# Dilated attention: the dense result's reload and a head's first merge weight tied to their program place

## The chip, the cores and the metric

The kernel runs on one core of a Trainium2 chip (trn2), as one program. The time is that of the whole program on the device, in microseconds (us), and lower is better. Engines are named as the profile names them: PE is TensorE (PEld its weight loads), ACT ScalarE, DVE VectorE, POOL GpSimd, SP SyncE. Each engine runs its own instructions in a fixed order; a queue that issues DMAs (transfers) belongs to an engine and stands in that same order.

## The reference

The whole kernel is a block of a transformer over 2048 positions: projections of the input, a differential attention of 4 heads, a dilated attention of 8 heads of width 64, an output projection, and then a second block with sliding-window attention. The change lies in the dilated attention. It computes, for each head, three banded attentions whose keys stand 1, 4 and 16 positions apart, and mixes them by their softmax denominators:

```python
DIL_PATTERNS = ((128, 1), (512, 4), (2048, 16))

def dilated_attention(q, k, v, slopes):
    """Mixture of dilation patterns merged by their softmax denominators."""
    outs, lses = [], []
    for window, dilation in DIL_PATTERNS:
        o, lse = dilated_branch(q, k, v, slopes, window, dilation)
        outs.append(o)
        lses.append(lse)
    w = jax.nn.softmax(jnp.stack(lses, axis=0), axis=0)
    out = jnp.sum(w[..., None] * jnp.stack(outs, axis=0), axis=0)
    return out.astype(q.dtype)
```

## The kernel before

The kernel is written with a tile scheduler: the program is traced instruction by instruction, and the scheduler (`schedule_with_timeline_sim=True`) then puts the instructions of each engine in an order of its own, by an estimate of when each will be ready. Data dependences become semaphores. What a line of the program issues can therefore stand far from its place in the program.

The dilated attention is `phase_b2` (from L473), at about 1320 to 1735 us of the span. It runs a software-pipelined loop over n, 16 steps for each of 8 heads. A head has two results. The dense one ("nat": window 128, distance 1) has scores in L563, exponentials in L569, transposes in L603, a copy `d_pn` (L606), a split into high and low parts on POOL (L610, L611), the product with the values `d_vn` (L637), an evacuation by ACT (`d_ta`, L643), transposes back (L649) and a reduction on DVE (L650) into `d_o1`. The residue one ("res": the patterns of distance 4 and 16) has scores in L590, biases and minima in L593, exponentials in L595, transposes `d_tr` in L622, high parts `d_ph` on ACT (L624), low parts `d_pl` on DVE (L625), the product with `d_vr` (L733), and goes by the same evacuation and reduction into `d_o2`.

The two results have their rows in different orders. So the dense one takes a round trip through memory: `back_nat` stores it (L656, on ACT's queue) and `load_merge` reloads it in the order of the residue classes into `d_a1` (L660, on ACT's queue too), with four loads of a gate, `d_sz`, on SP's queue (L664). Then `weights` makes the merge weights out of the minima and sums of both results, with `d_mm` first (L685, DVE), and puts the merge's products on a list, from which the loop takes one per step: four products on POOL in L701, two sums in L718, two products with the gate in L719, and the stores L672.

In the program, head h is stored at step n = 16h + 21, reloaded at 16h + 33 (16h + 24 for the last head) and weighed at 16h + 38. The first sum of L718 is at step 16h + 42. `d_a1`, `d_sz` and `d_o2` have two buffers each, so that the reduction L650 of head h + 2 (step 16h + 47) writes where head h's `d_o2` was. The loads of the next head's keys and queries, of `d_vn` (L544) and of `d_vr` are issued on SP's queue at fixed steps of the loop. DMAs share a few semaphores, so one may be held back until an earlier one on the same semaphore has landed.

Of the kernel before, what the change touches and what calls it, by code (L numbers as in the profile page):

```python
# [11 lines left out]
ALU = mybir.AluOpType  # L12
# [4 lines left out]
P = 128  # L17
# [455 lines left out]
def phase_b2(tc, c, scr, nat_bias, res_bias, res_two):  # L473
    nc = tc.nc
    NS = 8 * NT
    with (
# [180 lines left out]

        def load_merge(h):
            a1 = op.tile([P, NT, 66], F32, name="d_a1")
            nc.scalar.dma_start(a1.rearrange("r (j g) w -> r j (g w)", g=4),  # L660
                                scr["o1"][h].rearrange("(j r g) w -> r j (g w)", r=P, g=4))
            sz = op.tile([P, NT, 64], F32, name="d_sz")
            for j in range(4):
                nc.sync.dma_start(sz[:, 4 * j:4 * j + 4], by_rows(scr["sz"][:, 512 + 64 * h:576 + 64 * h], j))  # L664
            mrg[h] = [a1, sz]

        def by_rows(ap, j):
            return ap[512 * j:512 * j + 512].rearrange("(r g) d -> r g d", g=4)

        def store_y(h, av):  # L670
            for j in range(4):
                nc.gpsimd.dma_start(by_rows(scr["y"][1 + h // 6][:, 64 * (h % 6):64 * (h % 6) + 64], j),  # L672
                                  av[:, 4 * j:4 * j + 4])

        def weights(h):
            a1, sz = mrg.pop(h)
            o2 = o2s[h]
            m2, l2 = m2s.pop(h)
            m1, l1 = a1[:, :, 64], a1[:, :, 65]

            def small(nm):
                return sp.tile([P, NT], F32, name=nm, bufs=2)

            mm, d1, d2, ll, lt = (small(nm) for nm in ("d_mm", "d_d1", "d_d2", "d_ll", "d_lt"))
            nc.vector.tensor_tensor(mm, m1, m2, ALU.min)  # L685
            nc.vector.tensor_sub(d1, mm, m1)
            nc.vector.tensor_sub(d2, mm, m2)
            nc.scalar.activation(d1, d1, AF.Exp)
            nc.scalar.activation(d2, d2, AF.Exp)
            nc.vector.tensor_mul(ll, l1, d1)  # L690
            nc.vector.tensor_mul(lt, l2, d2)
            nc.vector.tensor_add(ll, ll, lt)
            nc.vector.reciprocal(ll, ll)
            nc.vector.tensor_mul(d1, d1, ll)
            nc.vector.tensor_mul(d2, d2, ll)
            av = a1[:, :, 0:64]
            sd = op.tile([P, NT, 64], F32, name="d_sd", tag="d_o2") if h == 7 else None
            hs = (slice(0, NT // 2), slice(NT // 2, NT))

            def scale(x, ap, w):  # L700
                nc.gpsimd.tensor_mul(ap[:, x], ap[:, x], w[:, x].unsqueeze(2).broadcast_to([P, NT // 2, 64]))  # L701

            if h == 7:
                nc.gpsimd.tensor_mul(sd, sz, d2.unsqueeze(2).broadcast_to([P, NT, 64]))
                nc.vector.tensor_mul(av, av, d1.unsqueeze(2).broadcast_to([P, NT, 64]))
                nc.vector.tensor_mul(av, av, sz)

                def tail():
                    nc.vector.tensor_mul(o2, o2, sd)
                    nc.vector.tensor_add(av, av, o2)  # L710
                    store_y(h, av)

                later.append(tail)
                return
            later.extend([
                *[lambda x=x: scale(x, av, d1) for x in hs],
                *[lambda x=x: scale(x, o2, d2) for x in hs],
                *[lambda x=x: nc.gpsimd.tensor_add(av[:, x], av[:, x], o2[:, x]) for x in hs],  # L718
                *[lambda x=x: nc.gpsimd.tensor_mul(av[:, x], av[:, x], sz[:, x]) for x in hs],  # L719
                lambda: store_y(h, av),  # L720
            ])
# [27 lines left out]
        for n in range(NS + LEAD + LB + 12):  # L749
            r = n - LEAD  # L750
# [14 lines left out]
            for h in range(8):  # L765
                at = NT * (h + 1) + LN + DN + (BACK if h < 7 else 3)
                if n == at:
                    load_merge(h)
# [6 lines left out]
            for h in range(8):  # L775
                if n == NT * (h + 1) + (WT if h < 7 else LEAD + LB + DR + 3):
                    weights(h)
# [3 lines left out]
            h, t = divmod(n, NT)  # L781
# [592 lines left out]
```

## Time and profile before

| what | value |
|---|---|
| median of 3 runs | 3005.81 us (3000.62 to 3008.73) |
| the profiled execution | 2996.59 us |
| its span, first to last instruction | 2994.8 us |
| its mean granted TensorE clock | 0.985 |
| busy: PE, PEld, DVE, ACT, POOL | 97%, 82%, 60%, 52%, 41% |

All rows come from the one profiled execution, which is 9.2 us shorter than the median of the runs. Busy shares are means over the whole span, with stages of different limits in it. A row of a timeline gives start, duration, engine, line and operation, and in brackets how long the engine stood idle just before it and what it waited for. "DMA s_o<-d_o" is the store of the dense result, "DMA d_a<-s_o" its reload. The granted clock is given as a share of the full one, so 1.00 is 2.4 GHz and 0.50 is 1.2 GHz.

### The profile page before, as it was taken

The numbers are of one execution on the slowest core, as the hardware profiler recorded it, in microseconds if no ns is written. First come the engines' busy times: TensorE is split into PE (matmuls) and PEld (weight loads), VectorE is DVE, ScalarE is ACT, GpSimd is POOL, SyncE is SP. The second block draws the span as 40 slices with busy tenths as digits, with TensorE's granted clock in tenths as the row PEclk, the third lists the DMA queues.
The fourth block names the chain that finished last, engine by engine and source line by source line (L and its number), as shares of the span: only waits on it lengthen the run. The fifth ranks groups of instructions, "written<-read, shape, count | busy, mean of one in ns | idle before, by whom it ended". The sixth has DMA issues, their size and how long they took to land.

```text
span 2994.8 us, 45167 instructions
## 1 busy us (share of the span) xinstructions
PE 2891.2 (97%) x15554; PEld 2464.7 (82%) x15554; DVE 1802.8 (60%) x4607; ACT 1565.5 (52%) x3480; POOL 1240.2 (41%) x1156
## 2 busy tenths in 40 slices
PE   9999999999999999998898899999999999999998
PEld 7778888888788888888787778888788888888787
DVE  4115656522788889877676654444535756766755
ACT  5222333311688888877787642222345666666621
POOL 1110111101688888845676610000145665555421
PEclk9999999999999999999999899999999999999999
DMA  6653444414223322148666452322554343332452
GB/s 211 118 155 85 120 114 120 112 65 142 91 56 90 82 60 77 44 110 166 131 144 126 126 159 83 111 93 92 183 162 153 98 132 110 101 117 71 142 192 78
DMA packets 410645, 346.00 MB, mean 116 GB/s; under 512 B 89744, under 2 KB 356400, under 8 KB 408496
## 3 DMA queue, kind: packets, MB, share of 16 engines
q1 hardware_dynamic: 388000, 329.24, 39.3%
q10 hardware_dynamic: 20736, 8.65, 1.5%
q0 software_dynamic: 1680, 5.21, 0.7%
q8 instruction: 124, 2.03, 0.3%
q14 instruction: 105, 0.86, 0.1%
HBM read 227.51 MB, written 116.52 MB: 115 GB/s over the span
## 4 chain that ended last, share of the span: by engine, by line
PE 85%; DMA 6%; DVE 3%; ACT 2%; SPq 1%; issue 1%; POOL 1%; ACTq 0%; DVEq 0%; POOLq 0%
PE psm L190 8%; PE psm L192 8%; PE psm L191 8%; PE s_ps L331 7%; PE e_mm L803 5%; PE e_mm L805 5%; PE e_mm L804 5%; PE c_mm L803 4%; PE c_mm L804 4%; PE c_mm L805 4%; PE t_ps L375 3%; DMA s_o<-d_o 2%; PE o_ps L389 2%; PE o_ps L391 2%; PE o_ps L390 2%; PE f_mm L804 2%
## 5 line engine op out<-in xcount | busy, mean ns | idle before, releaser
L190 PE MATMUL psm<-w,hh 128*128 128x512 f32 x1024 | 406.1, 398 | 9.8 <-DVE t L111 8.0
L191 PE MATMUL psm<-w,hl 128*128 128x512 f32 x1024 | 399.9, 392 | 0.0
L192 PE MATMUL psm<-w,hh 128*128 128x512 f32 x1024 | 399.8, 393 | 0.0
L101 POOL TENSOR_TENSOR w<-wraw,w 128x512 fp32r<-128x512 f32 x64 | 81.7, 1296 | 599.0 <-ACT w L100 591.2
L365 POOL TENSOR_TENSOR et<-et 128x1024 f32<-128x1024 f32 x124 | 296.4, 2416 | 0.0
L331 PE MATMUL s_ps<-kst,qst 128*128 128x512 f32 x1024 | 289.3, 406 | 4.6 <-DVE mx L337 3.6
L347 ACT ACTIVATE et<-et,nm 128x2048 f32<-128x2048 f32 x128 | 257.3, 2010 | 5.2
L1025 POOL TENSOR_TENSOR e_wt<-e_raw,e_wt 128x1024 fp32r<-128x1024 f32 x80 | 191.3, 2399 | 111.5 <-ACT e_wt L1024 110.6
L190 PEld LDWEIGHTS psm<-w,hh 128*128 128x128 f32 x1024 | 193.5, 189 | 48.6 <-DVE t L111 8.4
L803 PE MATMUL e_mm<-e_x,e_wt 128*128 128x512 f32 x576 | 228.2, 396 | 1.1 <-DVE e_k L1067 0.9
L805 PE MATMUL e_mm<-e_x,e_wt 128*128 128x512 f32 x576 | 226.9, 394 | 0.0
L192 PEld LDWEIGHTS psm<-w,hh 128*128 128x128 f32 x1024 | 193.1, 189 | 40.8
L804 PE MATMUL e_mm<-e_x,e_wt 128*128 128x512 f32 x576 | 226.6, 393 | 0.0
L191 PEld LDWEIGHTS psm<-w,hl 128*128 128x128 f32 x1024 | 193.7, 189 | 38.3
L331 PEld LDWEIGHTS s_ps<-kst,qst 128*128 128x128 f32 x1024 | 176.2, 190 | 43.8 <-DVE mx L337 17.7
L1126 POOL TENSOR_SCALAR e_es<-e_es,e_l 128x256 f32<-128x256 f32 (+1 forms) x256 | 118.4, 481 | 170.6 <-DVE e_l L1124 108.5
L364 POOL TENSOR_SCALAR et<-et,cc 128x1024 f32<-128x1024 f32 x124 | 138.6, 1134 | 109.2 <-PE psm L192 57.1
L377 DVE TENSOR_TENSOR ptl<-t_ps,pth 128x512 fp32r<-128x512 f32 x256 | 169.2, 684 | 17.6 <-ACT pth L376 17.1
L337 DVE CUSTOM_DVE_ANT_0 et<-s_ps,nd,mx 128x1024 f32<-128x1024 f32 x128 | 163.8, 1280 | 26.5 <-PE s_ps L331 24.6
L1113 DVE CUSTOM_DVE_ANT_0 e_es<-e_s,e_bias,e_sk 128x256 f32<-128x256 f32 (+1 forms) x256 | 117.4, 472 | 102.7 <-PE e_s L1105 71.3
L376 ACT ACTIVATE pth<-t_ps 128x512 fp32r<-128x512 f32 x256 | 143.8, 596 | 42.7 <-PE t_ps L375 39.0
L337 DVE CUSTOM_DVE_ANT_0 et<-s_ps,nd 128x1024 f32<-128x1024 f32 x128 | 156.1, 1219 | 14.3 <-PE s_ps L331 7.0
(268 smaller groups left out, 7727.6 us busy)
## 6 DMA issues: line engine op xcount, KB each, us to landing
e_raw<-in_a_w_in_dram SPq DMA_DIRECT2D x80, 512.0 KB, 3.6
wraw<-in_w_in_dram SPq DMA_DIRECT2D x64, 256.0 KB, 3.5
kst<-s_dk SPq DMA_DIRECT2D x128, 128.0 KB, 4.0
s_xt<-c_at SPq DMA_DIRECT2D x32, 512.0 KB, 6.9
e_x<-s_xt SPq DMA_DIRECT2D x32, 512.0 KB, 7.7
t<-in_x_dram SPq DMA_DIRECT2D x32, 256.0 KB, 5.6
s_dv<-t SPq DMA_DIRECT2D x32, 256.0 KB, 3.2
s_bv<-t SPq DMA_DIRECT2D x32, 256.0 KB, 3.7
```

The lines of the kernel that those rows point to most:

```text
L190: nc.tensor.matmul(ps, ah, cur[k][:, 0], start=k == 0, stop=False)
L191: nc.tensor.matmul(ps, al, cur[k][:, 0], start=False, stop=False)
L192: nc.tensor.matmul(ps, ah, cur[k][:, 1], start=False, stop=k == KD - 1)
L331: nc.tensor.matmul(ps[:, b * 512:b * 512 + 512], lhs, heads[h, "k", e, i, 2 * hf + b], start=i == 0, stop=i == 1)
L337: nc.vector.tensor_tensor_reduce(et[:, hf], ps, bias[:, off:off + 1024], 1.0, -3.0e38 if hf == 0 else mx[:, 0:1], ALU.add, ALU.max, mx[:, ...
L347: nc.scalar.activation(ev, ev, AF.Exp, bias=nm, scale=slope, accum_out=st[g]["l"][:, e:e + 1])
L365: nc.gpsimd.tensor_sub(es[0][:, hf], es[0][:, hf], es[1][:, hf])
L377: nc.vector.tensor_sub(tl[:, :, qi], pt, th[:, :, qi].bitcast(F32))
L803: nc.tensor.matmul(ps, ah, bh, start=first, stop=False)
L804: nc.tensor.matmul(ps, al, bh, start=False, stop=False)
L805: nc.tensor.matmul(ps, ah, bl, start=False, stop=last)
L1025: nc.gpsimd.tensor_sub(w[:, 1], raw, w[:, 0].bitcast(F32))
```

## The change

Two calls are wrapped in `tc.keep_in_program_order`: the reload of the dense result in `load_merge` and the first merge weight in `weights`. A wrapped instruction stays behind everything that the program issues before it on its own engine; no wait for data comes with that. Both kernels have the same instructions. The scheduler lays the others out around the two, so the order changes on all engines, from head 0's reload on.

```diff
--- before.py
+++ after.py
@@ -657,8 +657,9 @@
 
         def load_merge(h):
             a1 = op.tile([P, NT, 66], F32, name="d_a1")
-            nc.scalar.dma_start(a1.rearrange("r (j g) w -> r j (g w)", g=4),
-                                scr["o1"][h].rearrange("(j r g) w -> r j (g w)", r=P, g=4))
+            tc.keep_in_program_order(nc.scalar.dma_start(
+                a1.rearrange("r (j g) w -> r j (g w)", g=4),
+                scr["o1"][h].rearrange("(j r g) w -> r j (g w)", r=P, g=4)))
             sz = op.tile([P, NT, 64], F32, name="d_sz")
             for j in range(4):
                 nc.sync.dma_start(sz[:, 4 * j:4 * j + 4], by_rows(scr["sz"][:, 512 + 64 * h:576 + 64 * h], j))
@@ -682,7 +683,7 @@
                 return sp.tile([P, NT], F32, name=nm, bufs=2)
 
             mm, d1, d2, ll, lt = (small(nm) for nm in ("d_mm", "d_d1", "d_d2", "d_ll", "d_lt"))
-            nc.vector.tensor_tensor(mm, m1, m2, ALU.min)
+            tc.keep_in_program_order(nc.vector.tensor_tensor(mm, m1, m2, ALU.min))
             nc.vector.tensor_sub(d1, mm, m1)
             nc.vector.tensor_sub(d2, mm, m2)
             nc.scalar.activation(d1, d1, AF.Exp)
```

On ACT, this is what stands from head 2's store L656 on before (names end in the buffer's number; `s_o1_2` is head 2's place in memory, `d_er` and `d_ph` are the residue result's exponentials and high parts):

```order
L656 DMA s_o1_2_94<-d_o1_14743 128x16x66
L643 ACTIVATE d_ta_15564<-d_or_15533 128x512
L624 ACTIVATE d_ph_15608<-d_tr_15610 128x3x128
L624 ACTIVATE d_ph_15608<-d_tr_15639 128x4x128
L595 ACTIVATE d_er_15664,d_l2_15429<-d_er_15664,d_m2_15428 128x512
L595 ACTIVATE d_er_15709,d_l2_15429<-d_er_15709,d_m2_15428 128x384
L624 ACTIVATE d_ph_15608<-d_tr_15676 128x4x128
L606 ACTIVATE d_pn_15602<-d_tn_15597 128x512
L660 DMA d_a1_15968<-s_o1_2_94 128x4x264
L624 ACTIVATE d_ph_15608<-d_tr_15712 128x3x128
```

And with the change, from the same store on, and round the reload:

```order
L656 DMA s_o1_2_94<-d_o1_14743 128x16x66
L624 ACTIVATE d_ph_15608<-d_tr_15610 128x3x128
L624 ACTIVATE d_ph_15608<-d_tr_15639 128x4x128
L643 ACTIVATE d_ta_15564<-d_or_15533 128x512
L606 ACTIVATE d_pn_15672<-d_tn_15667 128x512
L624 ACTIVATE d_ph_15608<-d_tr_15676 128x4x128
...
L595 ACTIVATE d_er_15993,d_l2_15429<-d_er_15993,d_m2_15428 128x384
L527 ACTIVATE d_rb1__13772<-d_rb0_13765 128x896
L624 ACTIVATE d_ph_15887<-d_tr_15955 128x4x128
L660 DMA d_a1_15968<-s_o1_2_94 128x4x264
L595 ACTIVATE d_er_16013,d_l2_16009<-d_er_16013,d_m2_16008 128x384
```

The reload stood 8 rows behind its store and now stands 36 behind it, past the slope-scaled bias of a later head (L527).

On DVE, the place of head 2's first merge weight `d_mm_16146` before (L593 and L566 take the biases and minima of the residue and the dense scores, `d_o1_15323` is head 3's dense result):

```order
L593 ISA d_er_15850,d_m2_15428<-d_sr_15847,d_rb1__13772 128x384
L593 ISA d_m2_15428 128x1
L566 ISA d_en_15838,d_o1_15323<-d_sn_15837,d_nb1__13770 128x256
L566 ISA d_o1_15323 128x1
L685 TENSOR_TENSOR d_mm_16146<-d_a1_15968,d_m2_14848 128x16
L686 TENSOR_TENSOR d_d1_16147<-d_mm_16146,d_a1_15968 128x16
L687 TENSOR_TENSOR d_d2_16148<-d_mm_16146,d_m2_14848 128x16
L650 TENSOR_REDUCE d_o1_15323<-d_ob_15683 128x4x64
```

With the change, where lines from L662 of before on count one more (L685 is L686). `d_o2_15895` is head 3's residue result:

```order
L650 TENSOR_REDUCE d_o2_15895<-d_ob_16035 128x4x64
L625 TENSOR_TENSOR d_pl_16028<-d_tr_16099,d_ph_16027 128x4x128
L593 ISA d_er_16216,d_m2_16008<-d_sr_16213,d_rb0__13771 128x512
L593 ISA d_m2_16008 128x1
L625 TENSOR_TENSOR d_pl_16028<-d_tr_16134,d_ph_16027 128x3x128
L686 TENSOR_TENSOR d_mm_16146<-d_a1_15968,d_m2_14848 128x16
L566 ISA d_en_16277,d_o1_15903<-d_sn_16276,d_nb0__13769 128x256
...
L687 TENSOR_TENSOR d_d1_16147<-d_mm_16146,d_a1_15968 128x16
L688 TENSOR_TENSOR d_d2_16148<-d_mm_16146,d_m2_14848 128x16
```

The weight stood in front of a reduction of head 3's dense result; it now stands behind a reduction of head 3's residue result, 58 rows further on.

On POOL, the end of the stage before: head 6's merge (`d_a1_18249`) and the last splits of the loop (`d_nl_18177`), with the next stage's weight splits (L796):

```order
L701 TENSOR_TENSOR d_a1_18249<-d_a1_18249,d_d1_18345 128x8x64 x2
L701 TENSOR_TENSOR d_o2_17635<-d_o2_17635,d_d2_18346 128x512 x2
L610 TENSOR_SCALAR d_nh_18176<-d_pn_18174 128x512
L796 TENSOR_TENSOR c_wo3_0_18496<-c_raw_18494,c_wo3_0_18496 128x512
L718 TENSOR_TENSOR d_a1_18249<-d_a1_18249,d_o2_17635 128x8x64 x2
L611 TENSOR_TENSOR d_nl_18177<-d_pn_18174,d_nh_18176 128x512
L610 TENSOR_SCALAR d_nh_18176<-d_pn_18232 128x512
L719 TENSOR_TENSOR d_a1_18249<-d_a1_18249,d_sz_18251 128x8x64 x2
L849 TENSOR_TENSOR c_yn_18564<-c_yn_18564,ssq_sub_67 128x512
L796 TENSOR_TENSOR c_wo7_0_18516<-c_raw_18514,c_wo7_0_18516 128x512
L611 TENSOR_TENSOR d_nl_18177<-d_pn_18232,d_nh_18176 128x512
L672 DMA s_y_128_140<-d_a1_18249 512x1x64 x4
```

And with the change, where `d_a1_17708` is head 5's merge:

```order
L611 TENSOR_TENSOR d_nl_18177<-d_pn_18174,d_nh_18176 128x512
L673 DMA s_y_384_139<-d_a1_17708 512x1x64 x2
L611 TENSOR_TENSOR d_nl_18177<-d_pn_18232,d_nh_18176 128x512
L797 TENSOR_TENSOR c_wo7_0_18516<-c_raw_18514,c_wo7_0_18516 128x512
L702 TENSOR_TENSOR d_a1_18249<-d_a1_18249,d_d1_18345 128x8x64 x2
L702 TENSOR_TENSOR d_o2_17635<-d_o2_17635,d_d2_18346 128x512 x2
L719 TENSOR_TENSOR d_a1_18249<-d_a1_18249,d_o2_17635 128x8x64 x2
L720 TENSOR_TENSOR d_a1_18249<-d_a1_18249,d_sz_18251 128x8x64 x2
L673 DMA s_y_128_140<-d_a1_18249 512x1x64 x4
```

Head 6's products have moved from before the last split to behind it.

## Rows read from the trace of the kernel before

**Rows 1.** The profile's page, part 1: each engine's busy us, share of the span, instructions.

```profile
PE 2891.2 (97%) x15554; PEld 2464.7 (82%) x15554; DVE 1802.8 (60%) x4607; ACT 1565.5 (52%) x3480; POOL 1240.2 (41%) x1156
```

**Rows 2.** Chain of waits, 1330 to 1740 us: start us, us, what.

```profile
1480.45 10.92 DMA s_o<-d_o
...
1617.25 11.24 DMA s_o<-d_o
```

**Rows 3.** The store's line (L656), then the reload's (L660): time to landing.

```profile
DMA to landing us min/median/max: 6.0/10.7/11.2
DMA to landing us min/median/max: 3.6/3.7/5.0
```

**Rows 4.** Waits from 1435 to 1660 us, ScalarE, VectorE, TensorE: total us, times, longest.

```profile
ACT d_ph L624 <- DMA s_o<-d_o: 12.6, 2, 6.5
ACT d_er L595 <- DMA s_o<-d_o: 10.8, 2, 5.4
...
ACT d_ta L643 <- DMA s_o<-d_o: 5.1, 1, 5.1
...
ACT d_ta L643 <- DMA d_vn<-s_bv: 0.8, 1, 0.8
...
DVE d_mm L685 <- DMA d_a<-s_o: 21.0, 4, 6.9
...
PE d_tr L622 <- DVE d_pl L625: 11.3, 6, 5.9
```

**Rows 5.** Timeline of head 2: start us, us, engine, line, operation, [idle before <- releaser].

```profile
1476.12 0.60 PE L622 MATMUL d_tr<-id,d_er 128*128 128x128 f32 x4
...
1491.88 0.49 ACT L624 ACTIVATE d_ph<-d_tr 128x384 fp32r<-128x384 f32 x1 [6.54 <-DMA s_o<-d_o]
...
1493.11 1.09 PE L622 MATMUL d_tr<-id,d_er 128*128 128x128 f32 x4 [5.89 <-DVE d_pl L625]
```

**Rows 6.** Windows round the five reloads: us, each engine's busy us (count), clock, DMA, GB/s.

```profile
1435.00:1455.00 20.00, 13.65 (x89) 12.67 (x88) 10.01 (x32) 12.46 (x36) 7.65 (x9) 0.86 0.81 141
1480.00:1500.00 20.00, 13.91 (x79) 12.99 (x78) 9.01 (x30) 11.06 (x32) 9.51 (x12) 0.83 0.74 132
1527.00:1545.00 18.00, 13.21 (x77) 12.20 (x76) 9.45 (x30) 11.53 (x37) 7.65 (x8) 0.91 0.78 117
1571.00:1590.00 19.00, 14.05 (x81) 12.61 (x80) 10.44 (x35) 11.55 (x35) 8.58 (x10) 0.91 0.73 111
1616.00:1636.00 20.00, 15.04 (x85) 13.38 (x83) 9.83 (x33) 12.88 (x39) 7.16 (x8) 0.91 0.79 108
sum 97.00, PE 69.86 PEld 63.84 DVE 48.74 ACT 59.48 POOL 40.55; mean PE 13.97 PEld 12.77 DVE 9.75 ACT 11.90 POOL 8.11
```

**Rows 7.** Windows between them: same columns, first and last of five, and the sum.

```profile
1455.00:1480.00 25.00, 24.89 (x164) 23.36 (x163) 19.89 (x64) 22.50 (x64) 19.86 (x25) 0.98 0.48 109
...
1636.00:1660.00 24.00, 23.47 (x170) 22.68 (x171) 19.59 (x65) 21.54 (x63) 20.91 (x22) 1.00 0.30 77
sum 128.00, PE 125.65 PEld 118.98 DVE 103.29 ACT 116.70 POOL 114.42; mean PE 25.13 PEld 23.80 DVE 20.66 ACT 23.34 POOL 22.88
```

**Rows 8.** Windows from each dense store to the next, heads 1 to 5: the sum.

```profile
sum 224.91, PE 195.43 PEld 182.77 DVE 151.97 ACT 176.09 POOL 154.93; mean PE 39.09 PEld 36.55 DVE 30.39 ACT 35.22 POOL 30.99
```

**Rows 9.** Timeline of head 0's store (1386.95) and reload (1394.60), ScalarE behind each.

```profile
1387.44 0.60 ACT L643 ACTIVATE d_ta<-d_or 128x512 f32<-128x512 f32 x1 [4.55 <-DMA d_vn<-s_bv]
...
1395.07 0.60 ACT L643 ACTIVATE d_ta<-d_or 128x512 f32<-128x512 f32 x1 [1.83 <-DMA s_o<-d_o]
```

**Rows 10.** Timeline of the stage's end.

```profile
1696.00 0.58 PE L637 MATMUL d_or<-d_nl,d_vn 128*128 128x256 f32 x1 [3.59 <-POOL d_nl L611]
...
1713.09 0.80 PE L803 MATMUL c_mm<-c_wo,c_at 128*128 128x512 f32 x1 [3.94 <-DVE d_o L650]
```

**Rows 11.** The merge on GpSimd, tile d_a: count, ns min/median/max, first and last start us.

```profile
L701 POOL TENSOR_TENSOR d_a<-d_a,d_d x14: 1043/1045/1503, 1405.9 to 1678.6; 128x512 f32<-128x512 f32 x14
L718 POOL TENSOR_TENSOR d_a<-d_a,d_o x14: 1179/1192/1212, 1410.5 to 1685.5; 128x512 f32<-128x512 f32 x14
```

## The prediction

> **What bounds the kernel now.** I read, in this order: busy times, the chain of waits over the dilated stage, the waits by engine, a timeline of one head, and two sets of windows. The page's first part gives TensorE 97% of the span [rows 1]. If that held in this stage too, taking a wait from ScalarE would bring nothing, so the stage has to be looked at by itself. Its chain of waits shows the same piece once in each head of the steady part: the store of the dense result, 10.92 us from 1480.45 in head 2, 11.24 us from 1617.25 in head 5, and the like in all five heads from 1435 to 1660 us [rows 2]. A store is on the chain only if something stands until it has landed. The landing times are 10.7 us median for the store (11.2 at most) and 3.7 for the reload behind it [rows 3].
>
> Who stands there? Between 1435 and 1660 us ScalarE waits for that store under three names, 12.6 + 10.8 + 5.1 = 28.5 us in five waits, one per head; VectorE waits 21.0 us in four waits for the reload; and TensorE stands 11.3 us behind VectorE's low parts (L625), which wait for ScalarE [rows 4]. The timeline of head 2 shows how the waits hang together: some five microseconds after the store ScalarE reaches the reload (L660), and can issue it only when the store has landed; the evacuation behind it in the same queue starts at 1491.88 after 6.54 us of idling, and TensorE goes on after 5.89 us of its own [rows 5]. So the reload costs little itself: it blocks the in-order queue it stands in.
>
> The four transposes at 1493.11 then take 1.09 us [rows 5], where four took 0.60 in quiet stretches. The granted clock says why: in windows round the five reloads it is 0.83 to 0.91, in the windows between them 0.98 to 1.00 [rows 6, 7]. TensorE fell to its lower level (1.2 of 2.4 GHz) after it had stood idle.
>
> **The change part by part.** No instruction is added, removed or resized. Two are bound to their program place, and the scheduler lays out all engines anew from there.
>
> The reload. In program order it comes 12 steps of the loop after its store. A head is 16 steps and lasts 224.91 / 5 = 45.0 us [rows 8], so even at the 38 us that I come to below, 12 steps are 28 us. The store needs 11.2 at most [rows 3]. The order shows 34 to 52 ScalarE rows between the two, of 64 or so in a head, where 8 to 11 were: at 38 us a head at least 20 us. ScalarE's wait goes in heads 0 to 6; head 7's pair stays two rows apart.
>
> What it is worth, for the five heads of 1435 to 1660 us, counted in three ways:
> - By idle time and clock: the windows round the reloads last 97.00 us with TensorE busy 69.86, so 27.1 idle [rows 6]; in the quiet ones it is 128.00 - 125.65 = 2.35 of 128, or 1.8% [rows 7]. Less that usual share (1.8 us), 25.3 us go. The mean clocks of the five windows lack 0.14, 0.17, 0.09, 0.09 and 0.09 of 20, 20, 18, 19 and 20 us, together 11.3; weighted with the busy share 0.72, 8.2 us. Sum 33.5.
> - By pace: the quiet windows do 879 matmuls in 128 us, 0.1456 us each. The 411 of the others would take 59.8 us at that pace instead of 97, a gain of 37.2 [rows 6, 7].
> - As a floor: only ScalarE's waits, 28.5 us [rows 4].
>
> I take 34: the first names each part, and the second allows for no difference between the matmuls of both stretches. A head then lasts 45.0 - 6.8 = 38.2 us, against 176.09 / 5 = 35.2 us of ScalarE's work and 195.43 / 5 = 39.1 of TensorE's, of which about 1.6 was half-clock time [rows 8]. It fits, barely.
>
> On the clock term the Trainium skill ("TensorE: Matmul & The Clock Gate", "HAM oscillation — how this bites in real kernels") counts half of all throttled time as lost. By that, an estimate, the term would be 11.3 and the first sum 36.6. The trace speaks for less: idle time at the lower level loses nothing, and it is already counted as idle.
>
> The first merge weight (L685). Its 21.0 us of waiting go, since it now stands five steps (12 us) behind a reload that lands in 3.7. VectorE has room (151.97 / 5 = 30.4 us per head, rows 8). I add nothing: its wait lay beside ScalarE's.
>
> Heads 0 and 6, the tail. Head 0's reload held ScalarE 1.83 us [rows 9]; I add 1. Head 7's store, reload and merge are chained by data in either order. TensorE stands there 3.59 us for the last split on GpSimd and 3.94 us for a VectorE reduction that was queued behind the blocked first weight [rows 10]. In the new order that reduction stands ahead of the weight, and head 6's merge behind the last split instead of in front of it, so up to 7.5 us of idling could go. But head 6's merge (4 x 1.045 + 2 x 1.192 us for its first six products, rows 11) then ends later, and the output projection can't start before the merges land, so the end of the chain is where it was: I take 0, with -4 to +4.
>
> New waits? Several DMAs share a semaphore, so the store may wait for an earlier transfer. In the five heads this cost 0.8 us once [rows 4], which is the low bound per head; head 0's store shows the high one, ScalarE idle 4.55 us behind a load of the value tiles [rows 9]. I take the low one, as those loads are issued from the same program place as before. The reload itself now has only loads issued some seven steps earlier to share with. SyncE gets the merge's four other loads later, behind the key and query loads, where nobody is waiting.
>
> Sum: 34 + 1 + 0 = 35 us. The profiled execution (2996.59 us, its span 2994.8) would become 2961.6. The median of the runs shown is 3005.81, 9.2 above it, so I forecast 3005.81 - 35 = 2971.
>
> **The rivals.**
> *The wait moves to the store* (0.16). If each store waited for a value load as head 0's does, ScalarE would idle 4.55 us a head instead of 28.5 / 5 = 5.7. At today's loss of 34 / 5 = 6.8 us for 5.7 of waiting that is 5.4 a head, 27 of the 35 given back: 2998. Against it: 0.8 us once in five heads. For it: a new order can move it in front of a landing.
>
> *Nothing much happens* (0.06), because ScalarE and GpSimd are nearly full without the waits: 116.70 and 114.42 of 128 us in the quiet windows [rows 7]. Work waited off would come back as queueing: 3003 or so. Against it: in those same windows TensorE is busy 98%; they are the proof that 25 us can run without holes.
>
> *More than I say* (0.08). If TensorE's floor is its weight loads, 182.77 / 5 = 36.6 us a head [rows 8], there are 5 x (45.0 - 36.6) = 42 us to be had: 2964. The Trainium skill ("Perfetto Trace Analysis", "Identifying the Most-Contended Engine") calls matmul busy time a poor measure of the distance from the roofline and wants the weight loads' share. Here that is 118.98 of 128 us in the quiet windows [rows 7], so 93% where matmuls show 98%; against more gain stands that ScalarE's 35.2 are hardly less.
>
> *Slower: the merge comes too late on GpSimd* (0.06). The merged residue result has two buffers, so the first reduction of head h+2 (L650, step 47 counted from head h) waits until GpSimd has done head h's sums (L718, step 43). Before, the merge could start as soon as the reload landed; now it is held to step 38. Four steps are 9.5 us at 38 us a head. The six products up to there take 6.6 us [rows 11] among 31 us of GpSimd work a head [rows 8]. From 9.5 us of delay on VectorE is held, and all behind it. At a delay of 17 us it would cost 7.5 a head and some 1.6 of clock, 46 in five heads less the 35 won: 3017. Against it: GpSimd would be 81% busy, and in program order its work is spread one product per step.
>
> **How the numbers follow.** The forecast's chance is 0.64; its own range is a gain of 26 to 43 us (the 28.5 floor less a tail of 4, to 37.2 + 1 + 4), 2963 to 2980. The range to hold the time 8 times in 10 takes in the larger gain and the lighter half of the moved wait: 2958 to 2992. About 0.3%, 9 us, can be told from no change. Faster by more than that: the forecast, the larger gain and most of the moved wait, 0.64 + 0.08 + 0.11 = 0.83. Within it: the rest of the moved wait and the null, 0.05 + 0.06 = 0.11. Slower: 0.06.
>
> **What would show it.** Right: no wait of ScalarE for the dense store between head 0 and head 6, and none of VectorE for the reload; heads of 37 to 39 us from store to store; a granted clock near 1.00 in the whole stretch; everything up to 1390 us as before and the later stages of equal length. The moved wait would show as ScalarE waiting for value loads in front of each store; the late merge as VectorE's reduction waiting for GpSimd's sum. I am wrong if heads still last over 42 us, or if they are short and the time comes back between the last head and the output projection.

## The result

The change took the median from 3005.94 to 2964.93 us (four runs each), a ratio of 0.9864 with a 95% interval of 0.9841 to 0.9886: 41.0 us less, 34 to 48 by the interval. 2971 was predicted, a gain of 35. The profiled execution took 2958.66 us against the 2996.59 of before, 37.9 less.

### The profile after

The page's first lines for the kernel with the change. TensorE's share is 97% as before [rows 1]: its busy time and the span both fell, and the share does not show where.

```profile
span 2956.9 us, 45164 instructions
...
PE 2878.8 (97%) x15554; PEld 2455.2 (83%) x15554; DVE 1803.7 (61%) x4607; ACT 1562.5 (53%) x3480; POOL 1239.1 (42%) x1156
```

The chain of waits from 1330 to 1740 us, which had the dense store five times in heads 1 to 5 [rows 2], has it twice, in heads 3 and 4 (start us, us, what):

```profile
1508.61 11.07 DMA s_o<-d_o
...
1549.72 11.69 DMA s_o<-d_o
```

The times to landing, first of the store (L656), then of the reload (L660). In this execution the store takes as long as it did [rows 3]; what has changed is who stands until it lands:

```profile
DMA to landing us min/median/max: 6.4/11.0/12.4
DMA to landing us min/median/max: 3.7/6.4/9.3
```

The waits of ScalarE, VectorE and TensorE in heads 1 to 5, 1425 to 1625 us (total us, times, longest), the largest of each. ScalarE's 28.5 us for the store and VectorE's 21.0 us for the reload [rows 4] are gone. Of TensorE's waits, 29.1 us in all before (the 11.3 of [rows 4] and the lines below), 5.2 are left.

```profile
PE d_ob L649 <- ACT d_ta L643: 9.6, 3, 4.5
PE d_sn L563 <- DVE d_o L566: 3.8, 3, 2.7
PE d_tn L603 <- ACT d_pn L606: 3.7, 1, 3.7
```

There is one new wait for a transfer: VectorE's dense scores (L566) wait for the store, 7.8 us in two places. ScalarE's exponentials (L569) stand behind them. After:

```profile
ACT d_en L569 <- DVE d_o L566: 8.2, 5, 3.0
ACT d_ph L624 <- PE d_tr L622: 4.8, 11, 0.9
...
DVE d_er L593 <- PE d_tr L622: 17.0, 25, 1.9
DVE d_en L566 <- DMA s_o<-d_o: 7.8, 2, 4.1
...
PE d_sn L563 <- DVE d_o L566: 3.9, 4, 1.7
PE d_sr L590 <- DVE d_m L593: 0.7, 2, 0.4
```

That new wait on the timeline, at head 3's store. The scores of head 5 write their minima into `d_o1`, which has two buffers; head 3's store still reads the one they want:

```profile
1508.61 0.37 ACTq L656 DMA_DIRECT2D s_o<-d_o  x1
...
1519.81 0.42 DVE L566 CUSTOM_DVE_ANT_0 d_en<-d_sn,d_nb__13770 128x256 f32<-128x256 f32 x1 [3.70 <-DMA s_o<-d_o]
...
1520.64 0.73 PE L563 MATMUL d_sn<-d_k,d_q 128*128 128x256 f32 x4 [1.69 <-DVE d_o L566]
```

In the kernel before, ScalarE stood until the store had landed, and VectorE never waits there in heads 1 to 5; with that wait taken away this one appears, and TensorE idles 1.69 us behind it.

Where did the time go? Five windows cut at the stores of heads 0, 1, 6 and 7 and at the end of the stage, before (columns as in rows 6: us, busy us and count of each engine, clock, DMA share, GB/s):

```profile
1386.95:1435.04 48.09, 44.27 (x261) 39.93 (x262) 33.56 (x103) 40.19 (x113) 36.88 (x44) 0.89 0.54 126
1435.04:1659.95 224.91, 195.43 (x1272) 182.77 (x1271) 151.97 (x480) 176.09 (x495) 154.93 (x177) 0.95 0.64 131
1659.95:1700.38 40.43, 33.09 (x208) 29.20 (x207) 28.08 (x68) 29.12 (x71) 31.10 (x30) 0.94 0.45 125
1700.38:1728.91 28.53, 21.62 (x89) 17.27 (x88) 16.02 (x22) 7.52 (x15) 11.77 (x8) 0.79 0.61 181
1728.91:2994.80 1265.89, 1241.63 (x6332) 1042.10 (x6330) 715.00 (x2013) 580.00 (x1376) 430.15 (x524) 0.99 0.38 121
```

and after:

```profile
1386.16:1425.01 38.85, 37.77 (x258) 35.74 (x257) 29.98 (x90) 35.29 (x100) 22.76 (x28) 1.00 0.62 134
1425.01:1625.05 200.04, 194.46 (x1304) 183.15 (x1304) 158.85 (x501) 180.82 (x514) 158.93 (x182) 0.99 0.76 147
1625.05:1662.21 37.16, 31.18 (x203) 27.95 (x203) 31.78 (x71) 27.61 (x70) 30.99 (x30) 0.91 0.54 150
1662.21:1690.68 28.47, 24.17 (x92) 19.51 (x91) 13.76 (x22) 7.58 (x15) 20.01 (x19) 0.76 0.70 199
1690.68:2956.90 1266.22, 1241.26 (x6328) 1041.57 (x6326) 714.87 (x2013) 579.66 (x1376) 431.27 (x524) 1.00 0.38 121
```

The stage's tail (28.53 and 28.47 us) and everything behind it (1265.89 and 1266.22 us) have not moved. From head 0's store to head 7's the time fell from 313.43 to 276.05 us, by 37.4 of the 37.9. The stores stand a little earlier or later among the matmuls than they did, so the same window holds other work. Per matmul, heads 1 to 5 took 224.91 us for 1272 and now take 200.04 us for 1304, which is 195.1 us for 1272: 29.8 us less.

That size is one execution's. The kernel with the change was profiled a second time ("The new wait", below); there heads 1 to 5 took 195.61 us for the same 1304 matmuls, 190.8 for 1272, so 34.1 us less:

```profile
1426.78:1622.39 195.61, 192.70 (x1304) 181.54 (x1304) 158.77 (x501) 180.58 (x513) 159.30 (x182) 1.00 0.75 151
```

Nor are matmuls alike: among the 32 more in the new window are 13 of the long ones of L590, so the count per matmul makes the gain a little too small. The second profile also allows a comparison of like with like. From head 0's store to head 7's it holds the same 1739 matmuls as the kernel before, form by form. Before, and then the second profile:

```profile
1386.95:1700.38 313.43, 272.78 (x1739) 251.89 (x1740) 213.61 (x650) 245.40 (x677) 222.91 (x250) 0.94 0.60 129
1385.43:1659.54 274.11, 260.67 (x1739) 243.58 (x1740) 217.75 (x650) 243.03 (x677) 213.42 (x240) 0.98 0.69 146
```

That is 39.3 us less: TensorE's idle time fell from 40.65 to 13.44 us, by 27.2, and its busy time by 12.1.

### The profile page after: what moved, and what is told of

It reads as the page before. It is cut to its first block, busy times and chain, and to the rows that moved or that the text cites. A ratio compares the mean times of both kernels' runs of the same rounds, so it can differ in the third digit from the quotient of the medians.

```text
span 2956.9 us, 45164 instructions
## 1 busy us (share of the span) xinstructions
PE 2878.8 (97%) x15554; PEld 2455.2 (83%) x15554; DVE 1803.7 (61%) x4607; ACT 1562.5 (53%) x3480; POOL 1239.1 (42%) x1156
## 4 chain that ended last, share of the span: by engine, by line
PE 86%; DMA 5%; DVE 3%; ACT 2%; SPq 1%; issue 1%; POOL 0%; DVEq 0%; ACTq 0%; POOLq 0%
PE s_ps L331 8%; PE psm L190 7%; PE psm L192 7%; PE psm L191 7%; PE e_mm L804 5%; PE e_mm L806 5%; PE e_mm L805 5%; PE c_mm L804 4%; PE c_mm L805 4%; PE c_mm L806 4%; PE t_ps L375 3%; PE o_ps L389 2%; PE o_ps L391 2%; PE o_ps L390 2%; PE d_sr L590 2%; PE f_mm L805 2%
## 5 line engine op out<-in xcount | busy, mean ns | idle before, releaser
L192 PEld LDWEIGHTS psm<-w,hh 128*128 128x128 f32 x1024 | 192.9, 189 | 40.9
L191 PEld LDWEIGHTS psm<-w,hl 128*128 128x128 f32 x1024 | 193.7, 189 | 38.2
L850 POOL TENSOR_TENSOR c_yn<-c_yn,ssq_sub 128x512 f32<-128x512 f32 x16 | 17.0, 1061 | 354.1 <-DMA c_yn<-s_y 354.1
```

What stands on the lines that cost most here:

```text
L191: nc.tensor.matmul(ps, al, cur[k][:, 0], start=False, stop=False)
L192: nc.tensor.matmul(ps, ah, cur[k][:, 1], start=False, stop=k == KD - 1)
```

## The experiments

Theory A was the prediction's: the price was ScalarE's queue, blocked at the reload, and VectorE's wait lay beside it. Theory B: the price was VectorE's queue, blocked at the first weight. Theory C: any new order of the stage would have gained, since the old one was unlucky. The first four kernels below ran on one chip, on which the kernel before had a median of 2996.98 us; the other four ran on another, with 2999.39 us. So differences are compared, not times. The ranges of the first four expectations are times; they are read here as gains from the 3005.94 us of the result above, which the prediction started from within 0.2 us.

### The reload alone

```diff
-            tc.keep_in_program_order(nc.vector.tensor_tensor(mm, m1, m2, ALU.min))
+            nc.vector.tensor_tensor(mm, m1, m2, ALU.min)
```

> Only the reload is tied to its program place; the first weight is free. In the order the reload stands 38 to 52 ScalarE rows behind its store in heads 0 to 6, and the weight, which needs the reload, comes late by itself. Theory A (the price before was ScalarE's queue blocked at the reload): no wait of ScalarE for the dense store in heads 0 to 6, VectorE waits for the reload under 4 us in all, time 2958 to 2975 us. Theory B (the price was VectorE's queue blocked at the first weight, and its own tie is needed): VectorE still waits 15 us or more for the reload, time 2980 to 2995. Theory C (any new order of this stage would have gained as much): nothing said of waits, 2955 to 2985.

2958.82 us, 38.2 less than before; ratio 0.9873 (0.9858 to 0.9887), which can't be told from that of the whole change (0.9864). ScalarE has no wait for the dense store in heads 0 to 6. The weight came late by itself, as it needs the reload, but not quite late enough: theory A expected under 4 us of VectorE's waiting for the reload, and it was 12.6 in all eight heads, 7.0 of it in heads 1 to 5:

```profile
DVE d_mm L686 <- DMA d_a<-s_o: 7.0, 5, 3.4
```

What these waits cost can't be told: the gain is 2.8 us short of the whole change's 41.0, within the intervals. So no use of the second half of the change is shown when the first is there. Theory A's time holds here, and B's does not, but C's (a gain of 21 to 51 us) does too, and so would that of any theory in which both waits matter, since this edit removed most of both.

### The weight alone

```diff
-            tc.keep_in_program_order(nc.scalar.dma_start(
-                a1.rearrange("r (j g) w -> r j (g w)", g=4),
-                scr["o1"][h].rearrange("(j r g) w -> r j (g w)", r=P, g=4)))
+            nc.scalar.dma_start(a1.rearrange("r (j g) w -> r j (g w)", g=4),
+                                scr["o1"][h].rearrange("(j r g) w -> r j (g w)", r=P, g=4))
```

> Only the first weight is tied; the reload is free, and stands 7 to 10 ScalarE rows behind its store again. Theory A: ScalarE waits for the store as before, 25 us or more in heads 1 to 5, VectorE's 21 us for the reload are gone and bring nothing, since they lay beside ScalarE's: 2997 to 3012 us. Theory B: those 21 us come back as time: 2975 to 2988. Theory C: 2960 to 2985 as with the whole change.

2982.34 us, 14.6 less; ratio 0.9947 (0.9927 to 0.9967). The waits of ScalarE and TensorE in heads 1 to 5:

```profile
ACT d_ph L624 <- DMA s_o<-d_o: 19.4, 3, 7.1
ACT d_er L595 <- DMA s_o<-d_o: 5.8, 1, 5.8
...
ACT d_pn L606 <- DMA s_o<-d_o: 3.0, 1, 3.0
...
PE d_tr L622 <- DVE d_pl L625: 8.7, 6, 3.4
PE d_tn L603 <- ACT d_pn L606: 7.1, 2, 4.1
```

ScalarE's waits are there as theory A said, 28.2 us, but the weight's wait was worth 14.6 us on top of them, where A gave it nothing (at most 9 as a gain). As a time, 2982.34 lies in the ranges of B and C, but the kernel before is 9 us faster on this chip; as gains, B's range is 18 to 31 us and C's 21 to 46, and 14.6 lies in neither. Neither A nor B stands as it was put. C falls: this order is new on all engines too, and has a third of the gain.

### The reload 4 and 8 steps behind the store

```diff
-BACK = 12
+BACK = 4
```

> The whole change, but the program puts the reload 4 steps behind the store in place of 12. In the order it stands 20 and 22 rows behind its store in heads 0 and 1, and 8 to 10 rows in heads 2 to 6, as before. Theory A: ScalarE's wait is gone in head 1 and stays in heads 2 to 5, at 5 us or more each; so four of the five heads keep their loss of some 6.8 us: 2986 to 3000 us. Theory C: 2955 to 2985.

2982.79 us, 14.2 less; ratio 0.9951 (0.9936 to 0.9966). As a time that is under theory A's range and in C's; as a gain it lies in A's (6 to 20 us) and outside C's (21 to 51). ScalarE's waits for the store from head 0's store to head 7's are four, one in each of heads 2 to 5; heads 0 and 1, whose reloads stood 20 and 22 rows behind, have none:

```profile
ACT d_pn L606 <- DMA s_o<-d_o: 19.1, 3, 6.9
...
ACT d_ph L624 <- DMA s_o<-d_o: 3.4, 1, 3.4
```

With `BACK = 8`:

> The whole change with the reload 8 steps behind the store: 36 and 38 rows in heads 0 and 1, 21 to 28 rows in heads 2 to 6, some 12 to 16 us at 38 us per 66 rows, against the store's landing of 11 to 12. Theory A: ScalarE waits under 2 us per head and under 5 in all, time within 7 us of the whole change, 2958 to 2972. Theory C: the same range. If 12 steps were needed for another reason than the landing, 2975 or more.

2958.43 us, 38.6 less; ratio 0.9868 (0.9853 to 0.9883). From head 0's store to head 6's, ScalarE has no wait for a store at all. So the place matters as far as the landing, and 12 steps have room to spare. Within one kernel (`BACK = 4`), heads 2 to 5, with 8 to 10 rows between store and reload, waited, and heads 0 and 1, with 20 and 22, did not. Head 6 has as few rows and no wait, but it had none in the kernel before either.

### ScalarE free, VectorE blocked

The last cell of the table: the kernel before, with the reload on SyncE's queue.

```diff
-            nc.scalar.dma_start(a1.rearrange("r (j g) w -> r j (g w)", g=4),
+            nc.sync.dma_start(a1.rearrange("r (j g) w -> r j (g w)", g=4),
```

> The kernel before with the reload on SyncE's queue in place of ScalarE's, nothing tied: ScalarE free, the weight as early as before, SyncE blocked in front of the d_vr loads. Theory A with what the run with the weight alone showed (either queue costs when it is blocked alone): no wait of ScalarE for the store; VectorE waits 4 us or more per head for the reload, and now nothing covers it: 2972 to 2992 us. Theory F (only ScalarE's queue matters, a VectorE wait of this size is absorbed): 2955 to 2970. If blocking SyncE costs, waits for d_vr or later loads and over 2992.

2992.19 us, 7.2 less; ratio 0.998 (0.9971 to 0.9989). That is 0.2 us beyond A's range, where a cost of the blocked SyncE was to begin, but the sign named for that cost is missing: no engine waits for `d_vr` or a later load of the stage, but for 0.8 us behind `d_vn`, as before. Theory F falls. ScalarE never waits for the store. VectorE waits for the reload instead, and TensorE behind VectorE; heads 1 to 5:

```profile
DVE d_mm L685 <- DMA d_a<-s_o: 28.9, 5, 6.8
...
PE d_sn L563 <- DVE d_o L566: 14.7, 4, 5.6
PE d_tr L622 <- DVE d_pl L625: 6.0, 5, 4.4
```

Head 2 on the timeline: SyncE issues the reload, VectorE stands 4.14 us for it, and TensorE's next transposes run at the lower level (1.12 us, granted clock 0.50), just as they did behind ScalarE [rows 5]:

```profile
1487.11 0.39 SPq L660 DMA_DIRECT2D d_a<-s_o  x1
...
1490.97 0.18 DVE L685 TENSOR_TENSOR d_mm<-d_a,d_m 128x16 f32<-128x16 f32 x1 [4.14 <-DMA d_a<-s_o]
...
1493.37 1.12 PE L622 MATMUL d_tr<-id,d_er 128*128 128x128 f32 x4 [4.37 <-DVE d_pl L625]
```

And with the weight tied as well, so that only SyncE is blocked:

> The same with the first weight tied to its program place: ScalarE and VectorE free, only SyncE blocked, the reload itself as early as before. Theory A: nobody waits for the round trip but SyncE, whose next loads are not needed for some steps: as the whole change, 2953 to 2970 us. If the reload's early place in itself cost something (traffic beside the key loads), or SyncE's block did: 2975 or more.

2962.49 us, 36.9 less; ratio 0.9881 (0.9866 to 0.9895). No wait for the reload is left in heads 1 to 5 (VectorE's largest):

```profile
DVE d_er L593 <- PE d_tr L622: 15.9, 24, 1.9
DVE d_pl L625 <- ACT d_ph L624: 9.3, 9, 2.6
DVE d_en L566 <- PE d_tn L603: 5.1, 9, 1.1
DVE d_en L566 <- DMA s_o<-d_o: 5.1, 2, 2.8
```

This kernel differs from the one with the weight alone only in the queue of the reload, and gains 36.9 us where that gained 14.6. So the reload may stand this early, and a queue may be blocked by it, if nothing behind it in that queue is due. The whole change gained 40.9 us on this chip; the intervals overlap, so a small cost of the early place is not excluded.

The four cells, as the difference of medians on the same chip:

| | weight early | weight late |
|---|---|---|
| reload blocks ScalarE | 0 | -14.6 |
| ScalarE free | -7.2 | -36.9 (SyncE's queue), -38.2 (reload tied), -40.9 (whole change) |

Each wait alone costs most of what both cost together: of 37 to 41 us, 22 to 26 for ScalarE's and 30 to 34 for VectorE's. They run side by side, and VectorE's ends later, as the reload lands after the store (3.7 us later by the median of the kernel before [rows 3]).

### The new wait

> The whole change once more, for comparison on the same chip. 0.985 to 0.989 of the kernel before.

The whole change again: 2958.52 us, 40.9 less, ratio 0.9869 (0.9856 to 0.9883). VectorE's new wait is there once more, in heads 1 to 5:

```profile
DVE d_en L566 <- DMA s_o<-d_o: 6.5, 3, 2.8
```

The next run gives minima and sums a tile of their own:

```diff
...
+                mls[h] = op1.tile([P, NT, 2], F32, name="d_ml", bufs=3)
-            ml = o1s[h][:, t:t + 2, 64:66]
+            ml = mls[h][:, t:t + 2]
...
             if t == NT - 1:
+                nc.vector.tensor_copy(o1s[h][:, :, 64:66], mls.pop(h))
```

> The whole change, with the dense minima and sums in a small tile of their own (three buffers) that is copied into d_o1 just before the store, so that the dense scores of head h+2 no longer need head h's store to have landed. One small VectorE copy per head is added. In the trace of the change VectorE waits 7.8 us for the store in two places. Theory D (that wait is new, uncovered since ScalarE no longer stands until the store has landed, and it costs time): the waits go, 3 to 6 us faster than the whole change on the same chip. Theory E (it lies beside other work): within 2 us of it.

The wait is gone (VectorE's largest from 1425 to 1625 us, lines one later):

```profile
DVE d_er L594 <- PE d_tr L623: 17.4, 27, 1.7
DVE d_en L567 <- PE d_tn L604: 5.5, 10, 1.1
DVE d_pl L626 <- ACT d_ph L625: 5.5, 6, 1.3
```

From head 0's store to head 7's it took 272.3 us, against 274.1 in the second profile of the change and 276.05 in the first. The medians differ by 2.4 us (2956.16 and 2958.52): more than theory E's 2 and less than D's 3, and the intervals overlap. So neither is shown. If the new wait costs anything, it is some 2 to 4 us in the stage, and not to be told from nothing in the whole. This kernel has the lowest median of all that were run, by too little to be called faster than the change.

## Why the prediction was right

**The bound and the mechanism.** Right. The stage, not the kernel, had to be read; the queue blocked at the reload was the cost, and its waits left as predicted. Nearly all of the gain lies between the stores of heads 0 and 7: 37.4 and 39.3 us in the two profiles, where the sum was 35.

**The five heads, 34 us.** About right: 29.8 us per matmul in the first profile, 34.1 in the second. These are two executions of one kernel, 4.4 us apart in the five heads; the first has more of the new wait (7.8 us against 6.5) and a lower clock (0.99 against 1.00). Both terms fit. Idle: 224.91 - 195.43 = 29.5 us before, and 195.61 - 192.70 = 2.9 in the second profile, 2.8 for as many matmuls, so 26.6 us gone (24.0 by the first profile), where the term had 25.3. Clock: before, TensorE stood at its lower level in one stretch per head. Here are the first and the sum of the five:

```profile
1449.35:1456.15 6.80, 4.13 (x21) 4.01 (x20) 4.99 (x17) 5.39 (x18) 1.89 (x2) 0.50 0.13 44
sum 23.80, PE 17.72 PEld 16.58 DVE 12.71 ACT 20.05 POOL 9.64; mean PE 3.54 PEld 3.32 DVE 2.54 ACT 4.01 POOL 1.93
```

Of 23.80 us TensorE was busy for 17.72. At the full level that work would take 8 to 9 us less, an estimate from 1.09 and 0.60 us for four transposes [rows 5] and from half of 17.72. The term had 8.2.

The Trainium skill ("TensorE: Matmul & The Clock Gate", "HAM oscillation — how this bites in real kernels") counts half of all throttled time; by that, an estimate, the term would be 11.9. This trace speaks for less, as the prediction did with its 11.3: 6.1 of the 23.8 us were idle and are counted as such already.

The second count (37.2) is not excluded: it allows for no difference between matmuls, but so do 29.8 and 34.1, and like with like the stretch of all seven heads lost 39.3.

Two slips of the working change nothing: the row at 1491.88 is ScalarE's copy of high parts (L624), not the evacuation, and the lower end of the range adds up to 25.5, with the 1 us of head 0 in it.

**The signs named.** The waits are as forecast, but not every head lasts 37 to 39 us. Head 1 lasts over 42 in both profiles (44.95 and 44.76), which was named as a sign of being wrong:

```profile
1425.01:1469.96 44.95, 43.99 (x288) 40.86 (x288) 37.27 (x121) 41.45 (x121) 36.05 (x43) 1.00 0.70 144
```

It holds 288 matmuls, where heads 2 to 5 hold 253 to 264, and TensorE is busy for 98% of it at the full clock. So its length is work that the stores cut into it, not waiting. A limit per matmul would have been the better sign.

**"I add nothing" for the first weight.** The number was right, since the windows held both waits; the reason given was too weak. It lay beside ScalarE's wait, but that is no ground for thinking it free: with ScalarE alone set free, VectorE's wait came out of its cover and kept all but 7.2 us. Had the change moved the reload to another queue instead, the same reasoning would have forecast 35 us where 7 came.

**Heads 0 and 6, 1 us.** Too low: some 2 us each. Head 6's stretch lost 3.3 us, of which some 2.3 are left at 203 matmuls for 208. Head 0's went from 48.09 to 38.85, but not all by the change. Before its store ScalarE waits for a load of the value tiles in some executions and not in others: 4.55 us in the profile of before [rows 9], none in the first of the change, 4.2 in the second. The clock falls behind it. In the second profile the stretch took 41.35, for 236 matmuls where there were 261:

```profile
1385.43:1426.78 41.35, 37.48 (x236) 34.73 (x237) 27.29 (x80) 34.71 (x97) 23.14 (x29) 0.92 0.56 122
```

That is some 2 us less per 236 matmuls, against the 1.83 us that ScalarE stood at the reload [rows 9].

**The tail, 0 between -4 and +4.** Right: 28.53 and 28.47 us. TensorE no longer waits there for the reduction behind the blocked weight. In the first profile it waits 2.8 us for a load of the merged result instead, as the prediction argued. The wait for the last split, which lies in head 6's stretch, is still 3.3 us.

**The rivals.** The wait did not move to the store: no wait of ScalarE for a value load between 1425 and 1625 us. It did move, in small, to a place that no rival named, the scores' buffer. The late merge did not come: VectorE never waits for GpSimd's sum in those heads. Weight loads as the floor: they are busy 183.15 of 200.04 us in the first profile, 92%, and 181.54 of 195.61 in the second, 93%, where matmuls show 97% and 99%. The 42 us that this floor would have allowed were not reached.

## What to carry to other kernels

A DMA that must wait for another DMA should stand in its queue so far behind it that the landing is over, or in a queue where nothing behind it is due: the wait itself is cheap, the engine behind it is not. A scheduler may put it too early, and the profile then shows compute instructions that wait for a store they don't read. Before counting one of two engines' waits as covered by the other, ask what remains if only one goes: here either alone brought 7 to 15 us, and both 37 to 41.

## What was not expected of the hardware

In head 2 TensorE came back at the lower of its levels whichever engine had held it: four transposes took 1.09 us behind ScalarE's wait and 1.12 behind VectorE's, at a granted clock of 0.50 both times, where four took 0.60 in quiet stretches.

The times to landing vary between executions of one kernel as well as between kernels. The store's median is 10.7 us before, 11.0 and 9.9 in the two profiles of the change, and 8.5 to 10.3 in the other kernels. The reload's grew from 3.7 to 6.4 and 7.0 us with the change, and no engine waited for it in heads 1 to 5. Its later place alone does not explain that: 5.7 was measured with the weight alone, where the reload stands early, and 4.1 with `BACK = 8`, where it stands late. The cause is open.
